# One written order for VectorE and ScalarE over all heads of both halves, with the rotation of q and k in single steps

## The chip, the cores and the metric

The kernel runs on one core of one Trainium2 chip. The metric is the device time of one execution in microseconds. The time before is the median of 3 runs, 2492.38 us (2491.7 to 2492.94).

## What is computed

One decoder layer, batch 1, 1024 tokens, width 2048, all in float32. The reference, cut to what matters:

```python
hn = rmsnorm(h, norm_mix_g[i])
proj = hn @ w_in[i]                       # 2048 -> 8 x 1024 columns
sb_q, sb_k, sb_v, sb_g, df_q, df_k, df_v, df_g = jnp.split(proj, split_at, axis=-1)
# 8 stick-breaking heads: w = sigmoid(z) * prod over later keys of (1 - sigmoid(z)), out = w @ v
# 8 differential heads: rotary on a quarter of each q/k half, (softmax1 - lam * softmax2) @ v, rmsnorm
mixed = jnp.concatenate([sb_out * silu(sb_g), df_out * silu(df_g)], axis=-1)
h = h + mixed @ w_out[i]
gate = sigmoid(rmsnorm(h, norm_ple_g[i]) @ w_ple_gate[i])
h = h + gate * (p[i] @ w_ple_proj[i])
return rmsnorm(h, norm_final_g)
```

## The kernel before

**Products.** Every large product keeps float32 accuracy with two float32r parts of each operand, a high one (a copy) and a low one (the float32 value less the copy). Each product is three matmuls into one accumulator: high by high (L226), high by low (L227), low by high (L228). So each piece of weights costs ScalarE a copy (`whi`, L148), VectorE a subtraction (`wlo`, L149), and each block of the input the same (`xh` L1058, `xl` L1059).

**Stages.** The tokens are cut in two halves of 512 (half 1 holds the tokens that see half the keys). First the v and gate columns of the stick-breaking heads are made by a seven-product scheme (`Seven`, to about 340 us of the span). Then comes the head loop (L1048 to L1186, to about 1711 us): half 1, then half 0, each over heads 8 to 15 (differential) and then 0 to 7 (stick-breaking). Then follow the output projection, again by seven products, and the gated embedding.

**The head loop.** A `unit` (L212) is 4 pieces of weights by 2 column blocks by 4 input blocks: 32 ticks of three matmuls, into the accumulators `acc0` (done at tick 28) and `acc1` (done at tick 32). A differential head has two units (q and k, then v and gate), a stick-breaking head one (q and k; v and gate are loaded). The attention of a head runs beside the units of the next head. The class `Side` holds a list of steps with due ticks; `side.tick()` after each tick emits those that are due, in the order of their due times. `attention` returns such steps: `weights` (scores z by TensorE, mask L312, then for a stick head two sigmoids L328 and L329, a running product L335 and a product L340; for a differential head max L350, exponent L353, scaling L361, difference L366), `turn` (transposes, L398), `parts` (high copies L416 and L417, low subtractions `lead` L421 and `awl` L422), `mix` (the products with v, L440 to L445), `norm` (L485 to L497).

**Who sets the order.** TensorE's order is written by hand throughout. VectorE's and ScalarE's order is written by hand in the seven-product stage (`man2`) and in the stick-breaking heads of half 0 (`man3`, L1081). There `side.written` is true, and `side.later(dt, fn)` makes a step of its own of what else would be emitted at once. In all other heads (half 1, and the differential heads of half 0) the two engines are ordered by the compiler's scheduler from its own estimates. Each engine takes its instructions in order: one that waits holds all behind it.

**Names that the prediction uses.** `taken(c)` evicts accumulator c of q and k (`qk<-acc`, L1092 in stick heads, L1121 and L1123 in differential ones). In the written stick heads `taken(0)` is due at 28 and `taken(1)` at 31.5. The rotation of a differential head is L1125 to L1128 (shuffle, two products, sum) and then 6 or 8 copies and subtractions (L1132 to L1140), all emitted in one go. `tight` is head 15, the last differential head, whose steps are packed closer so that they end before the stick heads begin. At the change of halves the 16 blocks of the new half's input are loaded and split in one loop (L1054 to L1060) ahead of half 0's first head.

Of the kernel before, what the change touches and what calls it, by code (L numbers as in the profile page):

```python
# [13 lines left out]
F32 = mybir.dt.float32  # L14
# [6 lines left out]
P = 128  # L21
# [16 lines left out]
NORM_LAT = 11  # L38
LAM0 = 0.8 - 0.6 * math.exp(0.0)
# [8 lines left out]
def _body(ctx, nc, tc, ap):  # L48
# [226 lines left out]
    def attention(at, pz, half, hd, q, qz, K, KL, VV, sg, vf):  # L275
# [41 lines left out]
        def weights(rb, c):  # L317
# [30 lines left out]
            def one():  # L348
                mx = at.tile([P, 1], F32, name="mx", tag="mx", bufs=8)
                V.reduce_max(mx, z[:, vw], axis=AX.X, negate=True)  # L350
                et = at.tile([P, S], F32, name="et", tag="pt" if c else "bt", bufs=2 if c else 3)
# [75 lines left out]
        def mix(pr, g):  # L427
# [51 lines left out]
            side.later(4, low)  # L479

        def norm(pr):
# [20 lines left out]
            side.later(3, step)  # L502
# [12 lines left out]
        elif tight and half == 0:  # L515
            ss, t0, t1, tv, gap = [[0, 2], [4, 7], [10, 13], [30, 33]], 18, 42, 9, 4
        else:
            s0, s1, s2, t0 = ([0, 1], [3, 5], [7, 9], 16) if tight else ([0, 2], [5, 8], [12, 15], 19)
            gap = 4 if tight else gap
            last = t0 + gap * (n0 - 1)  # L520
            s3 = [last + 1, last + (3 if tight else 5)]
            ss = [s0, s1, s2, s3]
            t1 = s3[-1] + (13 if tight else LATD[half])
            tv = s1[-1] + 2
# [12 lines left out]
    with tc.tile_pool(name="at", bufs=2) as at, tc.tile_pool(name="pz", bufs=2, space=PSUM) as pz:  # L537
# [509 lines left out]
        side.add([(4, norms)])  # L1047
        for half in (1, 0):  # L1048
            tsl = slice(half * HALF, half * HALF + HALF)
            X = {}  # L1050
            if half == 1:
                X = X1
            else:
                for kt in KT:  # L1054
                    hi = xp.tile([P, HALF], F32R, name=f"xh{kt}", tag=f"xh{kt}")
                    lo = xp.tile([P, HALF], F32R, name=f"xl{kt}", tag=f"xl{kt}")
                    nc.sync.dma_start(lo.bitcast(F32), h_d[0, kt])
                    A.activation(hi, lo.bitcast(F32), AF.Copy, scale=gcol(kt))  # L1058
                    V.scalar_tensor_tensor(lo, lo.bitcast(F32), gcol(kt), hi.bitcast(F32), op0=ALU.mult, op1=ALU.subtract)  # L1059
                    X[kt] = hi, lo  # L1060
# [3 lines left out]
            for hd in (ORDER0, ORDER1)[half]:  # L1064
# [5 lines left out]
                if half == 0 and hd == H + 1:  # L1070
                    with tc.issue_after(lastsig[0].ins):
                        A.preload_act_table_set("natural_log_exp_and_others")
# [7 lines left out]
                if half == 0 and hd == 0:  # L1080
                    man3 = tc.manual_schedule(engines={V.engine, A.engine})  # L1081
                    man3.__enter__()
                    side.written = True
                if sb:
                    acc = [pp.tile([P, HALF], F32, name=f"acc{c}", tag="acc", bufs=2) for c in range(2)]
                    qk = [at.tile([P, 2, HALF], F32R, name="q", tag="q"), at.tile([P, 2, HALF + P], F32R, name="k", tag="k")]
                    rstd = rstds[half]

                    def taken(c, acc=acc, qk=qk, rstd=rstd):
                        f = f32t("qk")  # L1090
                        t = qk[c]
                        V.tensor_tensor(f, acc[c], rstd, op=ALU.mult)  # L1092
                        side.later(1, lambda: A.copy(t[:, 0, :HALF], f))
                        side.later(2, lambda: V.tensor_tensor(t[:, 1, :HALF], f, t[:, 0, :HALF].bitcast(F32), op=ALU.subtract))
# [3 lines left out]
                    unit(X, acc=acc, mid={2: load_vg})  # L1098
                    if not side.written:
                        taken(0)  # L1100
                        taken(1)
                    q, k = qk
                else:
                    acc = unit(X)
                rstd = rstds[half]
                if not sb:
                    q = at.tile([P, 2, HALF], F32R, name="q", tag="q")
                    k = at.tile([P, 2, HALF + P], F32R, name="k", tag="k")
                qz = None
                if not sb:  # L1110
                    if nqz[0] % 8 < 2:

                        qzs[nqz[0] % 2] = at.tile([P, 2, HALF], F32R, name="qz", tag="qz")
                        G.memset(qzs[nqz[0] % 2].bitcast(F32), 0.0)
                    qz = qzs[nqz[0] % 2]
                    nqz[0] += 1
                KL = None if sb else at.tile([P, 2, HALF], F32R, name="kl", tag="st")
                for c, t in () if sb else ((0, q), (1, k)):
                    f = f32t("qk")
                    if c == 0:  # L1120
                        V.scalar_tensor_tensor(f, acc[c], DF_SCALE, rstd, op0=ALU.mult, op1=ALU.mult)  # L1121
                    else:
                        V.tensor_tensor(f, acc[c], rstd, op=ALU.mult)  # L1123
                    sw = f32t("sw")
                    V.stream_shuffle(sw, f, SWAP)  # L1125
                    V.tensor_tensor(sw, sw, cs[:, 1, :], op=ALU.mult)
                    V.tensor_tensor(f, f, cs[:, 0, :], op=ALU.mult)
                    V.tensor_tensor(f, f, sw, op=ALU.add)  # L1128
                    for b in range(2):
                        r = slice(64 * b, 64 * b + 64)  # L1130
                        ro = slice(64 - 64 * b, 128 - 64 * b)
                        A.copy(t[r, b, :HALF], f[r])  # L1132
                        if c == 0:
                            A.copy(qz[r, b, :], f[r])
                            V.tensor_tensor(t[ro, b, :], f[r], t[r, b, :].bitcast(F32), op=ALU.subtract)
                        else:
                            A.copy(t[ro, b, :HALF], f[r])
                            V.tensor_tensor(KL[r, 0, :], f[r], t[r, b, :HALF].bitcast(F32), op=ALU.subtract)
                            for rr in (r, ro):
                                V.tensor_tensor(t[rr, b, HALF:], f[r, 3 * P:], t[r, b, 3 * P:HALF].bitcast(F32), op=ALU.subtract)  # L1140

                if sb:
                    vf, gf = vacc = vg
                else:
                    vacc = unit(X)
                    vf, gf = f32t("vf"), f32t("gf")
# [3 lines left out]
                def normed(i, t, vacc=vacc, rstd=rstd):  # L1150
                    V.tensor_tensor(t, vacc[i], rstd, op=ALU.mult)

                def gate(sg=sg, gf=gf, fast=fast):
# [6 lines left out]

                side.later(5, partial(normed, 0, vf))
                side.later(6, partial(normed, 1, gf))
                side.later(7, gate)
                side.later(10, lambda sg=sg, gf=gf: V.tensor_tensor(sg, sg, gf, op=ALU.mult))
                K = [k]
                VV = []
                if half == 1:
                    G.dma_start(k_d[hd].rearrange("p (a b) -> p a b", a=2), k[:, :, 0:HALF])
                    if not sb:
                        G.dma_start(kl_d[hd - H], KL[:, 0, :])  # L1170
                else:
# [17 lines left out]
        man3.__exit__(None, None, None)  # L1189
# [492 lines left out]
```

## Time and profile before

| what | value |
|---|---|
| median of 3 runs | 2492.38 us |
| the profiled execution's own time | 2487.77 us |
| its span, first to last instruction | 2486.0 us |
| mean granted TensorE clock | 0.994 |
| units of half 1, differential heads | about 337 to 734 us |
| units of half 1, stick-breaking heads | about 734 to 960 us |
| units of half 0, differential heads | about 960 to 1420 us |
| units of half 0, stick-breaking heads | about 1420 to 1711 us |

The busy rows of the page count the union of each engine's instructions. TensorE's matmuls overlap: one of 512 columns is shown with 0.39 us, and the next starts 0.227 us after it, so a busy share of 100% says only that no gap was longer than the overlap. A row of the view of waits names the waiting instruction and what released it, the total, the number of waits and the longest. In the timeline a row shows start, duration, engine, line, operation and tiles, and in brackets the idle time before it and what ended that. Back to back, VectorE's next instruction starts about 0.08 us before the end that the row of the one before shows, ScalarE's about 0.10 us, so the step from start to start is the duration less that.

### The profile page before, as it was taken

The page shows a single profiled execution, that of the slowest core. Times are in us where ns is not written, and L with a number is a line of the kernel's source. Part 1 is how long each engine was busy: PE and PEld are TensorE (multiplying, and loading weights), DVE is VectorE, ACT ScalarE, POOL GpSimd, SP SyncE. Part 2 cuts the span into 40 slices and gives each one's busy share as a digit, 9 for nine tenths or more (in the row PEclk, how much of TensorE's full clock was granted, in tenths as well). Part 3 has the DMA queues.
Part 4 walks back from the last instruction along what each step waited for, and adds up shares of the span by engine and source line. Part 5 has one row for each costly group of instructions (what it writes and reads, how often), then busy time and mean ns, then how long its engine had stood idle before and what let it go on. Part 6 is the DMA issues. An engine that isn't in the chain of part 4 may idle for free.

```text
span 2486.0 us, 31946 instructions
## 1 busy us (share of the span) xinstructions
PE 2404.7 (97%) x11434; PEld 1997.5 (80%) x11434; DVE 1794.5 (72%) x3010; ACT 1207.2 (49%) x2064; POOL 279.3 (11%) x361
## 2 busy tenths in 40 slices
PE   7999999999999999999999999998899999999997
PEld 5787878888888887888888878886787887787886
DVE  6888776778777778787878778878678674546555
ACT  5234344555565445555555555445423234546443
POOL 1211110000000001000000001110111113330110
PEclk9999999999999999999999999999999999999999
DMA  8786655444444556344444435556746777343433
GB/s 292 251 269 220 221 180 159 151 146 128 147 136 140 186 161 198 109 123 114 123 115 115 111 102 136 144 135 192 224 167 220 168 188 230 121 131 103 133 109 102
DMA packets 167471, 397.72 MB, mean 160 GB/s; under 512 B 18896, under 2 KB 23248, under 8 KB 167312
## 3 DMA queue, kind: packets, MB, share of 16 engines
q1 hardware_dynamic: 131040, 302.07, 38.3%
q0 software_dynamic: 36272, 93.60, 14.3%
q8 instruction: 90, 1.47, 0.3%
q14 instruction: 69, 0.57, 0.1%
HBM read 297.03 MB, written 106.95 MB: 163 GB/s over the span
## 4 chain that ended last, share of the span: by engine, by line
PE 81%; DVE 8%; DMA 5%; ACT 4%; issue 3%; SPq 0%; DVEq 0%; ACTq 0%
PE acc L226 16%; PE acc L227 16%; PE acc L228 16%; PE pbc L598 4%; PE pbc L596 4%; PE pbc L597 4%; PE tp L398 2%; PE pa L596 1%; PE pa L598 1%; PE pa L597 1%; PE z L305 1%; PE z L304 1%; PE av L445 1%; PE av L444 1%; PE av L443 1%
## 5 line engine op out<-in xcount | busy, mean ns | idle before, releaser
L226 PE MATMUL acc<-xh,whi 128*128 128x512 f32 x1568 | 628.8, 401 | 2.2 <-DVE gt L1295 1.5
L228 PE MATMUL acc<-xh,wlo 128*128 128x512 f32 x1568 | 613.9, 392 | 0.0
L227 PE MATMUL acc<-xl,whi 128*128 128x512 f32 x1568 | 613.5, 391 | 0.0
L149 DVE TENSOR_TENSOR wlo<-wraw,whi 128x1024 fp32r<-128x1024 f32 x252 | 312.6, 1240 | 230.4 <-ACT whi L148 224.8
L148 ACT CAST whi<-wraw 128x1024 fp32r<-128x1024 f32 x252 | 265.0, 1052 | 290.2 <-PE acc L227 255.8
L228 PEld LDWEIGHTS acc<-xh,wlo 128*128 128x128 f32 x1568 | 295.0, 188 | 63.6
L226 PEld LDWEIGHTS acc<-xh,whi 128*128 128x128 f32 x1568 | 296.0, 189 | 57.0 <-issue 2.2
L227 PEld LDWEIGHTS acc<-xl,whi 128*128 128x128 f32 x1568 | 296.2, 189 | 53.5 <-issue 0.2
L686 ACT CAST wpr<-T 128x512 fp32r<-128x512 f32 x128 | 78.1, 621 | 314.4 <-DVE T L644 310.1
L417 ACT CAST awh<-tp 128x256 fp32r<-128x256 f32 (+1 forms) x160 | 81.0, 506 | 108.7 <-PE tp L398 108.6
L353 ACT ACTIVATE et<-z,mx 128x512 f32<-128x512 f32 (+7 forms) x128 | 94.5, 738 | 61.3 <-DVE mx L350 55.3
L110 POOL TENSOR_TENSOR ssq<-ssq,sq 128x512 f32<-128x512 f32 x56 | 83.6, 1493 | 303.6 <-ACT sq L109 253.9
L422 DVE TENSOR_TENSOR awl<-tp,awh 128x256 fp32r<-128x256 f32 (+1 forms) x160 | 92.3, 577 | 31.5 <-ACT awh L417 30.7
L335 DVE TENSOR_TENSOR_SCAN st<-pt 128x511 f32<-128x511 f32 (+3 forms) x64 | 86.7, 1355 | 29.6 <-ACT pt L328 29.1
L350 DVE TENSOR_REDUCE mx<-z 128x1 f32<-128x512 f32 (+7 forms) x128 | 96.4, 753 | 1.4
L700 DVE TENSOR_TENSOR wpr<-T,wpr 128x512 fp32r<-128x512 f32 x128 | 87.7, 685 | 6.3 <-ACT wpr L686 4.5
L596 PE MATMUL pbc<-cS,wpr 128*128 128x512 f32 x224 | 87.5, 390 | 3.2 <-DVE u L1439 1.6
L598 PE MATMUL pbc<-cS,wpr 128*128 128x512 f32 x224 | 87.3, 390 | 0.0
L597 PE MATMUL pbc<-cS,wpr 128*128 128x512 f32 x224 | 87.3, 390 | 0.0
L328 ACT ACTIVATE pt<-z 128x512 f32<-128x512 f32 (+3 forms) x64 | 41.7, 651 | 89.6 <-DVE z L312 81.1
L445 PE MATMUL av<-awl,v 128*128 128x256 f32 x256 | 73.6, 287 | 7.6 <-DVE awl L422 7.6
L226 PE MATMUL acc<-cA11h,whi 128*128 128x512 f32 x192 | 76.2, 397 | 0.6 <-DVE qk L1092 0.6
(402 smaller groups left out, 5335.9 us busy)
## 6 DMA issues: line engine op xcount, KB each, us to landing
wraw<-w_in SPq DMA_DIRECT2D x192, 512.0 KB, 3.6
wraw<-w_gate SPq DMA_DIRECT2D x64, 512.0 KB, 3.6
wraw<-w_out SPq DMA_DIRECT2D x72, 256.0 KB, 3.6
wraw<-w_vg SPq DMA_DIRECT2D x71, 256.0 KB, 4.2
comb_d<-sg POOLq DMA_DIRECT2D x48, 256.0 KB, 7.1
spare<-xT SPq DMA_DIRECT2D x44, 256.0 KB, 3.9
xl<-h_d SPq DMA_DIRECT2D x40, 256.0 KB, 5.1
vghalf_d<-hc POOLq DMA_DIRECT2D x32, 256.0 KB, 4.3
```

The source lines that it names most:

```text
L148: side.later(1, lambda: A.copy(hi[:, o], raw[:, o]))
L149: side.later(4, lambda: V.tensor_tensor(lo[:, o], raw[:, o], hi[:, o].bitcast(F32), op=ALU.subtract))
L226: T.matmul(acc[c], hi[:, k2, kh, c, :], xh, start=first, stop=False)
L227: T.matmul(acc[c], hi[:, k2, kh, c, :], xl, start=False, stop=False)
L228: T.matmul(acc[c], lo[:, k2, kh, c, :], xh, start=False, stop=last)
L350: V.reduce_max(mx, z[:, vw], axis=AX.X, negate=True)
L353: A.activation(et[:, vw], z[:, vw], AF.Exp, bias=mx[:, 0:1], accum_out=l)
L422: V.tensor_tensor(wl[:, o, :], tp[:, o, :], wh[:, o, :].bitcast(F32), op=ALU.subtract)
L445: T.matmul(av, vv[:, 0, blk % 4, :], wl, start=False, stop=last)
L596: T.matmul(o, wh[:, w], xh, start=start and k == 0, stop=False, skip_group_check=True)
L597: T.matmul(o, wh[:, w], xl, start=False, stop=False, skip_group_check=True)
L598: T.matmul(o, wl[:, w], xh, start=False, stop=k == 3, skip_group_check=True)
```

## The change

All head-loop work of VectorE and ScalarE gets the written order: `man2` is no longer closed before the head loop but after it, `man3` goes, and `side.written` is set before the first head. What was emitted at once becomes steps:

- The rotation of a differential head becomes seven steps each for q and k at the due ticks `ROPE`, counted from the eviction; the last of q falls 15.5 ticks and the last of k 23 ticks after it. The two blocks of 64 rows have one step each for their low parts. q and k tiles are allocated at the eviction.
- A differential head's max and exponent are separate steps (`DF`).
- `wlo` is emitted at 3 in place of 4 after the piece's load.
- `taken(1)` is due at 31 in every head (before 31.5 in the written stick heads).
- The split of half 0's 16 input blocks is spread over the last unit of half 1: four times four steps, 4.5 ticks apart.
- Head 15 of half 1 gets the steps `[[0, 2], [4, 7], [10, 13], [22, 25]]` with `gap` 5 in place of `[[0, 1], [3, 5], [7, 9], ...]` with `gap` 4.
- The norm factors of both halves become steps at 1 and 3; `low` and `step` of the sub-norm move from 4 to 5 and from 3 to 4.

No arithmetic is added or left out, and the numbers of matmuls and of VectorE's instructions stay. The core of the diff:

```diff
+XLAT = 6
+DF = 1, 1.5, 4, 5.5
+WLO = 3
+ROPE = (1.5, 5, 7, 8.5, 12, 14, 15.5), (1.5, 13, 14.5, 16, 19.5, 21.5, 23)
...
-            side.later(4, lambda: V.tensor_tensor(lo[:, o], raw[:, o], hi[:, o].bitcast(F32), op=ALU.subtract))
+            side.later(WLO, lambda: V.tensor_tensor(lo[:, o], raw[:, o], hi[:, o].bitcast(F32), op=ALU.subtract))
...
-            def one():
+            def top():
                 mx = at.tile([P, 1], F32, name="mx", tag="mx", bufs=8)
                 V.reduce_max(mx, z[:, vw], axis=AX.X, negate=True)
+                side.later(DF[1], partial(one, mx))
...
-            side.later(1, one)
-            side.later(3, two)
+            side.later(DF[0], top)
+            side.later(DF[2], two)
             if c:
-                side.later(4.5, three)
+                side.later(DF[3], three)
...
         elif tight and half == 0:
             ss, t0, t1, tv, gap = [[0, 2], [4, 7], [10, 13], [30, 33]], 18, 42, 9, 4
+        elif tight:
+            ss, t0, t1, tv, gap = [[0, 2], [4, 7], [10, 13], [22, 25]], 17, 33, 9, 5
...
-        man2.__exit__(None, None, None)
+        side.written = True
...
-                rstd_from(ps, 1.0 / NK, eps6, EPS, ssa[hf], t)
+                side.later(1 if hf else 3, partial(rstd_from, ps, 1.0 / NK, eps6, EPS, ssa[hf], t))
...
+                    def swap(pc):
+                        for i, kt in enumerate((pc * 2, pc * 2 + 8, pc * 2 + 1, pc * 2 + 9)):
+                            side.add([(XLAT + 4.5 * i, load_x0(kt))])
+
+                    side.add([(8 * pc + 7, partial(swap, pc)) for pc in range(4)])
...
-                    if side.written:
-                        side.add([(28, partial(taken, 0)), (31.5, partial(taken, 1))])
+                    side.add([(28, partial(taken, 0)), (31, partial(taken, 1))])
+                    side.add([(36, partial(normed, 0)), (37, partial(normed, 1)), (38, gate), (41, gated)])
...
+                        steps = [lambda: V.stream_shuffle(sw, f, SWAP),
+                                 lambda: V.tensor_tensor(sw, sw, cs[:, 1, :], op=ALU.mult),
+                                 lambda: V.tensor_tensor(f, f, cs[:, 0, :], op=ALU.mult),
+                                 lambda: V.tensor_tensor(f, f, sw, op=ALU.add),
+                                 high, partial(low, 0), partial(low, 1)]
+                        side.add(zip(ROPE[c], steps))
...
         side.written = False
-        man3.__exit__(None, None, None)
+        man2.__exit__(None, None, None)
```

More of the change, by code (lines that the diff above doesn't have):

```diff
@@ L478, in mix @@
             side.later(3, squared)
-            side.later(4, low)
+            side.later(5, low)
         def norm(pr):
@@ L501, in norm @@
             side.later(1, roots)
-            side.later(3, step)
+            side.later(4, step)
         n0 = nb // 2
@@ L1079, in _body @@
                 vg = []
[L1080 to L1094, printed above, removed]
-                    if side.written:
-                        side.add([(28, partial(taken, 0)), (31.5, partial(taken, 1))])
[L1098 to L1146, printed above, removed]
+                rstd = rstds.get(half) if half == 0 or hd != ORDER1[0] else ssa[1]
+                qk = {}
+                if half == 1 and hd == ORDER1[-1]:
+                    def swap(pc):
+                        for i, kt in enumerate((pc * 2, pc * 2 + 8, pc * 2 + 1, pc * 2 + 9)):
+                            side.add([(XLAT + 4.5 * i, load_x0(kt))])
+                    side.add([(8 * pc + 7, partial(swap, pc)) for pc in range(4)])
@@ L1147, in _body, with store_k, two_accs @@
+                def store_k(hd=hd, qk=qk, half=half):
+                    if half == 1:
+                        G.dma_start(k_d[hd].rearrange("p (a b) -> p a b", a=2), qk[1][:, :, 0:HALF])
+                        if hd >= H:
+                            G.dma_start(kl_d[hd - H], qk["kl"][:, 0, :])
+                def two_accs():
+                    return [pp.tile([P, HALF], F32, name=f"acc{c}", tag="acc", bufs=2) for c in range(2)]
                 sg = at.tile([P, HALF], F32, name="sg", tag="sg", bufs=3)
@@ L1159, in gate, with gated, taken, low @@
                         A.activation(sg, sg, AF.Exp, scale=-1.0)
[L1161 to L1164, printed above, removed]
+                def gated(sg=sg, vg=vg):
+                    V.tensor_tensor(sg, sg, vg[1], op=ALU.mult)
+                acc = two_accs()
+                if sb:
+                    def taken(c, acc=acc, qk=qk, rstd=rstd, store_k=store_k):
+                        f = f32t("qk")
+                        if c == 0:
+                            t = at.tile([P, 2, HALF], F32R, name="q", tag="q")
+                        else:
+                            t = at.tile([P, 2, HALF + P], F32R, name="k", tag="k")
+                        qk[c] = t
+                        V.tensor_tensor(f, acc[c], rstd, op=ALU.mult)
+                        def low():
+                            V.tensor_tensor(t[:, 1, :HALF], f, t[:, 0, :HALF].bitcast(F32), op=ALU.subtract)
+                            if c:
+                                store_k()
+                        side.later(1, lambda: A.copy(t[:, 0, :HALF], f))
+                        side.later(2, low)
+                    def normed(i, vg=vg, rstd=rstd):
+                        V.tensor_tensor(vg[i], vg[i], rstd, op=ALU.mult)
+                    side.add([(28, partial(taken, 0)), (31, partial(taken, 1))])
+                    side.add([(36, partial(normed, 0)), (37, partial(normed, 1)), (38, gate), (41, gated)])
+                    unit(X, acc=acc, mid={2: load_vg})
+                    while 1 not in qk:
+                        side.tick()
+                    q, k, qz, KL = qk[0], qk[1], None, None
+                else:
+                    def taken(c, acc=acc, qk=qk, rstd=rstd, store_k=store_k):
+                        f, sw = f32t("qk"), f32t("sw")
+                        if c == 0:
+                            t = at.tile([P, 2, HALF], F32R, name="q", tag="q")
+                            if nqz[0] % 8 < 2:
+                                qzs[nqz[0] % 2] = at.tile([P, 2, HALF], F32R, name="qz", tag="qz")
+                                G.memset(qzs[nqz[0] % 2].bitcast(F32), 0.0)
+                            other = qk["qz"] = qzs[nqz[0] % 2]
+                            nqz[0] += 1
+                            V.scalar_tensor_tensor(f, acc[c], DF_SCALE, rstd, op0=ALU.mult, op1=ALU.mult)
+                        else:
+                            t = at.tile([P, 2, HALF + P], F32R, name="k", tag="k")
+                            other = qk["kl"] = at.tile([P, 2, HALF], F32R, name="kl", tag="st")
+                            V.tensor_tensor(f, acc[c], rstd, op=ALU.mult)
+                        qk[c] = t
+                        rows = [(slice(64 * b, 64 * b + 64), slice(64 - 64 * b, 128 - 64 * b)) for b in range(2)]
+                        def high():
+                            for b, (r, ro) in enumerate(rows):
+                                A.copy(t[r, b, :HALF], f[r])
+                                if c == 0:
+                                    A.copy(other[r, b, :], f[r])
+                                else:
+                                    A.copy(t[ro, b, :HALF], f[r])
+                        def low(b):
+                            r, ro = rows[b]
+                            if c == 0:
+                                V.tensor_tensor(t[ro, b, :], f[r], t[r, b, :].bitcast(F32), op=ALU.subtract)
+                                return
+                            V.tensor_tensor(other[r, 0, :], f[r], t[r, b, :HALF].bitcast(F32), op=ALU.subtract)
+                            for rr in (r, ro):
+                                V.tensor_tensor(t[rr, b, HALF:], f[r, 3 * P:], t[r, b, 3 * P:HALF].bitcast(F32), op=ALU.subtract)
+                            if b:
+                                store_k()
+                        steps = [lambda: V.stream_shuffle(sw, f, SWAP),
[4 more added lines that the diff above has]
+                        side.add(zip(ROPE[c], steps))
+                    side.add([(28, partial(taken, 0)), (31, partial(taken, 1))])
+                    unit(X, acc=acc)
+                    vacc = two_accs()
+                    def normed(i, vacc=vacc, vg=vg, rstd=rstd):
+                        vg.append(f32t(("vf", "gf")[i]))
+                        V.tensor_tensor(vg[i], vacc[i], rstd, op=ALU.mult)
+                    side.add([(28, partial(normed, 0)), (31, partial(normed, 1)), (33, gate), (37, gated)])
+                    unit(X, acc=vacc)
+                    q, k, qz, KL = qk[0], qk[1], qk["qz"], qk["kl"]
```

45 lines of the change are left out of this document (20 added, 25 removed).

## The prediction

> **What bounds the kernel now.** I read the page's busy rows first: TensorE covers 97% of the span, VectorE 72%.
>
> ```profile
> span 2486.0 us, 31946 instructions
> ...
> PE 2404.7 (97%) x11434; PEld 1997.5 (80%) x11434; DVE 1794.5 (72%) x3010; ACT 1207.2 (49%) x2064; POOL 279.3 (11%) x361
> ```
>
> The change leaves TensorE's instructions as they are, and their order too except in head 15 of half 1. So it can only remove TensorE's waits or add some. Where they are shows in the busy time by stretch (length, then busy time of TensorE, weight loads, VectorE, ScalarE, GpSimd; granted clock, DMA share, GB/s).
>
> ```profile
> 511.00:561.00 50.00, 50.00 (x241) 41.88 (x240) 38.09 (x85) 28.13 (x57) 1.76 (x3) 1.00 0.45 143
> 1447.80:1451.20 3.40, 3.40 (x12) 2.82 (x11) 1.99 (x4) 1.63 (x2) 2.27 (x3) 0.50 0.85 231
> 1547.00:1582.40 35.40, 34.89 (x190) 29.78 (x190) 28.39 (x39) 16.71 (x27) 3.75 (x5) 1.00 0.51 134
> ```
>
> In half 1's differential heads (first row) TensorE has no gap, and the view of waits lists none from 360 to 730 us or from 1000 to 1440. That is where the rotation stands: **its spreading has no wait to remove**. The third row is one stick head of half 0 with a gap of 0.5 us, the second a stretch at half clock after a long wait. The view of waits from 1440 to 1480 us (waiter, releaser, us in total, times, longest), then that from 1500 to 1700:
>
> ```profile
> PE av L440 <- DVE awl L422: 3.6, 1, 3.6
> PE av L440 <- DVE lead L421: 2.0, 1, 2.0
> ```
> ```profile
> PE av L440 <- DVE lead L421: 5.5, 5, 3.5
> ```
>
> The other waits in reach: 1.2 us at 738 (z L304 on the exponent L353, head 15 of half 1), 0.6 and 1.2 at 789 and 795, 4.0 in six waits at 951 to 996 (the change of halves), 1.0 at 340. From 340 to 1480 they sum to 1.0 + 1.2 + 1.8 + 4.0 + 5.9 = 13.9 us: the most that the change can win by waits, 0.6% of the time.
>
> **Stick heads of half 0: the reordered eviction.** These were already in written order, and the two programs' orders differ here in one point that matters: the eviction of acc1, due at 31 in place of 31.5. VectorE's rows before, in the head from 1534 us:
>
> ```profile
> 1532.10 0.69 DVE L1094 TENSOR_TENSOR q<-qk,q 128x512 fp32r<-128x512 f32 x1 [0.69 <-ACT q L1093]
> 1532.95 0.69 DVE L422 TENSOR_TENSOR awl<-tp,awh 128x512 fp32r<-128x512 f32 x1 [0.16 <-ACT awh L417]
> 1533.92 0.29 DVE L310 TENSOR_TENSOR zm<-z,masks 128x128 f32<-128x128 f32 x1 [0.28 <-PE z L302]
> 1534.24 0.30 DVE L312 TENSOR_TENSOR z<-z,zm 128x128 f32<-128x128 f32 x1
> 1534.60 0.69 DVE L1092 TENSOR_TENSOR qk<-acc,ssa 128x512 f32<-128x512 f32 x1
> 1535.37 1.49 DVE L335 TENSOR_TENSOR_SCAN st<-pt 128x639 f32<-128x639 f32 x1
> ...
> 1538.56 0.68 DVE L422 TENSOR_TENSOR awl<-tp,awh 128x512 fp32r<-128x512 f32 x1
> ...
> 1546.56 0.26 DVE L421 TENSOR_TENSOR lead<-tp,lead 128x128 fp32r<-128x128 f32 x1
> ```
>
> And TensorE's rows for the last matmul into acc1 and the two that wait further down:
>
> ```profile
> 1534.17 0.39 PE L228 MATMUL acc<-xh,wlo 128*128 128x512 f32 x1
> ...
> 1539.90 0.28 PE L445 MATMUL av<-awl,v 128*128 128x256 f32 x1
> ...
> 1546.88 0.39 PE L440 MATMUL av<-lead,v 128*128 128x256 f32 x1 [0.50 <-DVE lead L421]
> ```
>
> In the new order qk of acc1 stands right behind `q`, ahead of `awl`, `zm` and `z`. acc1 ends at 1534.17 + 0.39 = 1534.56, so VectorE, free at 1532.8, stands until 1534.6. Then qk takes a step of 0.60 (0.69 less 0.08), `awl` 0.61, so `zm` starts at 1535.8, `z` at 1536.1, done at 1536.4 in place of 1534.5: **1.9 us late**. Behind that mask wait ScalarE's sigmoid (before at 1534.64) and VectorE's scan, `k`, `wlo` and the second `awl`, back to back. That `awl` would end at 1539.24 + 1.9 = 1541.1, and TensorE wants it at 1539.90: it was 0.66 early and is 1.2 late. From there to `lead` VectorE has two idle gaps (0.85 and 0.51), but each waits for a ScalarE instruction whose own input moves too, so I let them take up nothing. `lead` is then 1.9 late where TensorE already waited; TensorE itself comes 1.2 later, so 0.7 comes on top. Sum 1.2 + 0.7 = **1.9 us a head**. With heads 2 to 5 alike that is 7.6. The first (`lead` at 1512, before just in time by 0.2) gives 1.7. In the last one both waits meet the 3.5 us wait at 1688: its `awl` at 1682 was just in time and is 1.7 late, its `lead` some 0.9: 2.6. Sum 1.7 + 7.6 + 2.6 = +11.9; bounds 0 (delay all absorbed) and 13.3 (seven heads by 1.9).
>
> **Hand-over to the stick heads (1459 to 1476).** Same eviction: before, qk of acc1 (1459.04) stood behind `zm` 1457.20, the mask and a max; now they stand behind it, so the exponent of 1458.78 comes some 2.4 later. `sql`, at whose row TensorE waited 0.3, ends 1.2 to 1.7 later, and the `lead` at 1475 some 0.7. Together +2.2; bounds 0 and 3.5.
>
> **Head 15.** In half 1 the steps are 2 to 3 ticks apart in place of 1 to 2: z is free in time, and the waits from 738 to 746 (1.2 gap, with its short successors 1.8) go: -1.8; bounds 0 and -2. In half 0 `lead` was late by 3.6 because `sql` (1435.74, after 1.33 idle), `wlo` (1.22) and `v` (0.69) stood ahead of the last keys' mask and max; in the new order mask and max stand ahead of `sql`, and the exponent starts about 1.33 + 1.2 = 2.5 earlier, the rest by the later difference L366 behind `wlo`: -3.2; bounds 0 and -3.6. With that wait goes the half-clock stretch behind it: 3.4 us at 0.50 is -1.7. The late sum is -4.9.
>
> **Start and change of halves.** At 337 the copy of the first piece's `whi` now stands behind four copies `xh` (0.72 each), and the second piece's `wlo` behind all six products of both norm factors (0.67 each) in place of three: TensorE would wait some 0.5, 0.8 and 1.7, and loses its 1.0 wait for the squares: +2.0; bounds -1 and +4. At the change of halves the splits (ScalarE 0.72, VectorE 0.74, sixteen each) no longer come in a lump but reach into the first head of half 0, where they stand among the last stick head's sigmoids and `lead`: the old 4 us of gaps (5.1 over the issue step) mostly go, and waits for z, two late blocks, one `wlo` and `lead` of some 7.5 come. +2.4; bounds -5.1 and +5, because it hangs on when loads land (median 5.1 us for this load). The heads of 789 and 795: +0.3; bounds ±1. Entry of the output projection, whose queue is some 0.5 longer: +0.5.
>
> **Steps at no cost.** `wlo` at 3 in place of 4 keeps its place behind `lead` in the stick heads; `low` and `step`, one tick later, feed the sub-norm of differential heads, where TensorE waits for nothing: 0, bound +0.5 each at head 15. SP's order changes by a dozen loads that move a few places, GpSimd's by one; k's stores are issued earlier. SP's longest wait is for `wlo` (901 us in 172 waits), so weights are loaded a piece ahead and a few places hide: 0, except at the change of halves, where it is in the bounds above.
>
> **Differential heads.** Nothing hides a gain here. As to loss: VectorE has 38.1 of 50 us, and the spread steps leave a `wlo` 1.0 us ahead of its use at the least: 0; bound +1 a head.
>
> **Sum** on the profiled execution: 11.9 + 2.2 - 1.8 - 4.9 + 2.0 + 2.4 + 0.3 + 0.5 = +12.6, taken as +13. That execution took 2487.77 us (span 2486.0 and 1.8 around it), 4.6 below the median of 2492.38; the median after is then **2505 us**.
>
> **A rule on the clock.** In this trace the granted clock is 0.50 for 3.4 us after the wait of 3.6 at 1443 and after that of 2.0 at 1473, and stays at 1.00 after 3.5 at 1688 and after 1.4 at 951. [...]
>
> **Rivals.**
> (1) *Faster: standing at the head of the queue reaches nobody.* Place: everything behind the acc1 eviction, the late `whi` and the spread splits. It decides by the slack ahead of TensorE's use: 0.66 us at `awl` (1539.90), nothing at `lead`. If VectorE and ScalarE made up all delays, only the removals stay: -1.8 - 4.9 - 5.1 = -11.8, 2481 us. Against it: the rows are back to back from 1534 to 1541. 8%.
> (2) *The delay runs out in the two gaps* of 0.85 and 0.51 us: six heads by 1.36 less, 2505 - 8 = 2497, on the border of what counts. For it: the gaps are there; against it: both end on ScalarE rows that move. 10%.
> (3) *The differential heads get waits,* one us in each of fifteen: 2520. For it: VectorE at 76% and in fixed order; against: 1 us of room. 7%.
> (4) *Half clock after the new waits:* eight waits of about 2 us, 1.7 each: 2519. For: the stretch after 2.0 us; against: none after 1.4 and 3.5. [...] 7%.
> The forecast keeps 68%.
>
> **Range and chances.** 2496 to 2516 reaches down to (2) and, upward, to the high bounds of hand-over and change of halves (+1.3 and +2.6) with the rule's 1.7 and some of the differential heads' loss; it leaves out (1), half of (3) and (4), and some edge. A measurement can tell about 0.2% (5 us). Faster 8% from (1); within 5 us 6%, half of (2) and 1% of the forecast; slower 86%.
>
> **What would show it.** Right: `av L440 <- DVE lead` in 1500 to 1700 grows from 5.5 to about 11 us, a new `av L445 <- DVE awl` appears there with some six waits of 1 to 2, the 3.6 us at 1443 is gone, and stretches of the differential heads stay at 50.00 of 50. Wrong: `awl` and `lead` waits unchanged in the stick heads, or gaps among the differential heads.

## The result, and the profile after

The changed kernel takes **2506.17 us** (median of 4 runs, 2502.95 to 2508.74), the kernel before on the same chip 2492.66 (4 runs): ratio 1.0052, 95% interval 1.0035 to 1.0069, so 13.5 us or 0.5% slower. The forecast was 2505. The profiled execution took 2504.36 us. Its busy rows, from the page of the changed kernel:

```profile
span 2502.6 us, 31959 instructions
...
PE 2411.7 (96%) x11434; PEld 1998.8 (80%) x11434; DVE 1810.6 (72%) x3010; ACT 1200.0 (48%) x2063; POOL 279.8 (11%) x361
```

The same numbers of matmuls and of VectorE instructions, 16.6 us more span: what was added is waiting, and some half clock. VectorE's 16 us more are no added work: the durations of its instructions sum to 1942.2 us before and 1941.5 after, but they overlap the end of the one before by 130.9 us in all, where it was 147.6. The busy time by stretch of the changed kernel (length, TensorE, weight loads, VectorE, ScalarE, GpSimd; granted clock, DMA share, GB/s) shows where:

```profile
511.00:561.00 50.00, 50.00 (x241) 41.87 (x240) 39.24 (x86) 27.67 (x56) 1.76 (x3) 1.00 0.45 143
...
1538.70:1576.00 37.30, 35.43 (x190) 29.81 (x190) 28.22 (x39) 16.72 (x27) 3.75 (x5) 1.00 0.48 127
1700.40:1707.20 6.80, 5.51 (x18) 4.74 (x19) 4.52 (x6) 0.99 (x2) 0.00 (x0) 0.50 0.37 101
```

The differential heads (first row) still have no gap. One stick head of half 0 (second row) now needs 37.3 us for the same 190 matmuls, of which TensorE is shown busy for 35.4; before it was 35.4 with 34.9. The third row is a stretch at half clock that the kernel before did not have there. The view of waits of the changed kernel from 1440 to 1480 us, then from 1500 to 1720:

```profile
PE av L447 <- DVE awl L429: 4.1, 2, 2.8
PE msq L492 <- ACT sqh L476: 1.3, 1, 1.3
```
```profile
PE av L447 <- DVE lead L428: 11.6, 6, 5.4
PE av L452 <- DVE awl L429: 5.3, 6, 1.4
```

The wait of 3.6 at 1443 is gone (now 1.25); in the stick heads `lead` has grown from 5.5 to 11.6, and there are six new waits for `awl`: the two rows that the forecast asked for. VectorE's timeline of the changed kernel in the head from 1533 us shows the mechanism, and TensorE's rows the two waits:

```profile
1533.28 0.69 DVE L1134 TENSOR_TENSOR qk<-acc,ssa 128x512 f32<-128x512 f32 x1 [1.80 <-PE acc L232]
1533.89 0.68 DVE L429 TENSOR_TENSOR awl<-tp,awh 128x512 fp32r<-128x512 f32 x1
1534.48 0.28 DVE L314 TENSOR_TENSOR zm<-z,masks 128x128 f32<-128x128 f32 x1
...
1539.13 0.68 DVE L429 TENSOR_TENSOR awl<-tp,awh 128x512 fp32r<-128x512 f32 x1
...
1547.12 0.26 DVE L428 TENSOR_TENSOR lead<-tp,lead 128x128 fp32r<-128x128 f32 x1
```
```profile
1539.87 0.39 PE L452 MATMUL av<-awl,v 128*128 128x256 f32 x1 [0.87 <-DVE awl L429]
...
1547.44 0.50 PE L447 MATMUL av<-lead,v 128*128 128x256 f32 x2 [1.00 <-DVE lead L428]
```

VectorE stands 1.80 us with the eviction at the head of its queue, until acc1 ends; `awl`, `zm` and all that follows come behind it, and TensorE waits 0.87 for the second `awl` and 1.00 for `lead`, where before it waited 0.50 in all.

**Where the time went.** TensorE's order is the same in both programs but for some matmuls of head 15, so the start of the same matmul can be compared. Chosen ones (us in the trace before, after, and the difference):

| matmul at | before | after | difference |
|---|---|---|---|
| end of the first seven products | 336.9 | 338.1 | +1.2 |
| first differential head | 361.7 | 363.8 | +2.1 |
| end of the differential heads of half 1 | 734.9 | 737.0 | +2.1 |
| first stick head of half 1 | 753.3 | 753.6 | +0.3 |
| second | 797.3 | 796.2 | -1.1 |
| first differential heads of half 0 | 1022.6 | 1022.2 | -0.4 |
| behind head 15's last `lead` | 1452.8 | 1448.4 | -4.3 |
| end of the hand-over | 1497.1 | 1493.1 | -4.0 |
| behind the first stick head | 1534.4 | 1533.1 | -1.3 |
| behind four more | 1676.2 | 1682.4 | +6.2 |
| in the last one | 1695.7 | 1708.2 | +12.5 |
| in the output projection | 1792.8 | 1809.2 | +16.4 |

The first +1.2 was there before the head loop, in a stage whose order the change leaves alone: 0.6 of it by 43 us, behind a stretch at half clock at 24 us that lasted 6.8 us in place of 3.4, the rest from 173 to 178 us.

### The profile page after: what moved, and what is told of

Its sections match the earlier page's. It is cut to its first block, busy times and chain, and to the rows that moved or that the text cites. A ratio compares the mean times of both kernels' runs of the same rounds, so it can differ in the third digit from the quotient of the medians.

```text
span 2502.6 us, 31959 instructions
## 1 busy us (share of the span) xinstructions
PE 2411.7 (96%) x11434; PEld 1998.8 (80%) x11434; DVE 1810.6 (72%) x3010; ACT 1200.0 (48%) x2063; POOL 279.8 (11%) x361
## 3 DMA queue, kind: packets, MB, share of 16 engines
q0 software_dynamic: 36272, 93.60, 14.2%
## 4 chain that ended last, share of the span: by engine, by line
PE 79%; DVE 10%; DMA 4%; ACT 4%; issue 3%; SPq 0%; DVEq 0%; ACTq 0%
PE acc L230 16%; PE acc L232 16%; PE acc L231 16%; PE pbc L606 4%; PE pbc L604 4%; PE pbc L605 4%; PE tp L405 2%; PE pa L606 1%; PE pa L604 1%; PE pa L605 1%; PE z L309 1%; PE z L308 1%; PE av L452 1%; PE av L451 1%; PE av L450 1%
```

## The experiments

**1. The eviction alone, from both sides.** First the changed kernel with the one number put back (in both halves' stick heads), then the kernel before with the one number changed:

```diff
-                    side.add([(28, partial(taken, 0)), (31, partial(taken, 1))])
+                    side.add([(28, partial(taken, 0)), (31.5, partial(taken, 1))])
```

> The changed kernel with one number put back: the stick heads' eviction of acc1 due at 31.5 in place of 31 (both halves). Theory: that eviction, at the head of VectorE's queue before acc1 is done, is what costs the stick heads of half 0 (+7.6 in four heads, +6.3 in the last, of +16.6 in all). Then `awl` and `lead` waits from 1500 to 1720 us fall from 5.3 and 11.6 us to about 0 and 5, and the time falls by 8 to 13 us, to 2493 to 2498. Rival: the stick heads lose to the whole of the new order around them (loads, weights' low parts a tick earlier, gate's product as steps of their own), of which the eviction is only one: then the waits stay above 12 us together and the time above 2503.

> The kernel before with that one number changed: 31 in place of 31.5 in the written stick heads of half 0, nothing else. Theory: the whole cost of the stick heads comes with it, so the time rises by 8 to 14 us, to 2500 to 2507, with an `awl` wait of some 0.9 and a `lead` wait of some 1.0 in each of the four middle heads. Rival: alone it costs nothing, because the order around it is the old one: 2492 to 2494 and `lead` still 5.5 us in 5 waits.

Measured: 2495.41 us, ratio to the kernel before 1.0006 (0.9995 to 1.0017); and 2506.99, 1.0059 (1.0046 to 1.0071). The waits from 1500 to 1720 us of the changed kernel with 31.5, then of the kernel before with 31:

```profile
PE av L447 <- DVE lead L428: 7.9, 6, 3.7
...
PE av L452 <- DVE awl L429: 0.7, 2, 0.4
```
```profile
PE av L440 <- DVE lead L421: 10.0, 5, 6.0
PE av L445 <- DVE awl L422: 5.7, 6, 1.4
```

The `awl` waits come and go with that number. By the same matmuls, each of the four middle heads becomes 1.87 us shorter in the one and 1.9 us longer in the other. Half 1's stick heads do not move by 0.1 us. The theory holds: without this number the whole rest of the change, in sum, costs nothing and wins nothing. One thing did not go as expected: `lead` fell to 7.9 and not to 5, and the hand-over's waits (4.1 and 1.3 at 1440 to 1480) stayed.

**2. The rotation in one go.**

```diff
-ROPE = (1.5, 5, 7, 8.5, 12, 14, 15.5), (1.5, 13, 14.5, 16, 19.5, 21.5, 23)
+ROPE = (1, 1, 1, 1, 1, 2, 2), (1, 1, 1, 1, 1, 2, 2)
```

> The changed kernel with q's and k's rotation not spread: the seven steps of each due within two ticks of the eviction, in place of 15.5 and 23. Theory: spreading removes no wait of the kernel before, which had none there, but it is what lets a fixed order have none. Emitted in a lump of some 17 VectorE instructions in a queue of fixed order, the lump stands ahead of the next `wlo` parts and of the mask; then new waits of TensorE for `wlo` come in every differential head, of 2 to 6 us, in all 30 to 65 us: 2535 to 2570. Rival: VectorE, busy 76%, makes it up before TensorE comes: 2504 to 2509, no waits from 360 to 730 us.

Measured: 2607.85 us, 1.0467 (1.0448 to 1.0485): 102 us more than the changed kernel, well above the expected range. Its waits from 360 to 730 us, and two stretches of one of its heads:

```profile
PE acc L232 <- DVE wlo L153: 39.3, 7, 5.8
```
```profile
425.00:430.30 5.30, 0.53 (x3) 0.11 (x1) 5.07 (x13) 3.28 (x7) 0.57 (x2) 1.00 0.00 0
430.30:437.10 6.80, 5.77 (x15) 4.61 (x16) 3.63 (x7) 2.14 (x4) 1.18 (x3) 0.50 0.92 277
```

In the first stretch TensorE stands, no DMA moves, and VectorE is busy for 5.07 of 5.30 us: it works off the lump, with `wlo` behind it. In the second the clock is 0.50 for 6.8 us. Each of the eight heads of half 1 loses 64.0 / 8 = 8.0 us, 5.7 by the wait and most of the rest by the clock. The clock was left out of the expectation; and the waits came at its upper end in every head of half 1 (in seven heads of half 0 they are 2.8). So the spreading has no wait of the kernel before to remove, but in a fixed order it is what keeps 100 us of waits and half clock away.

**3. The weights' low part at 4.** `WLO = 4` in place of 3 in the changed kernel.

> The changed kernel with the weights' low part due 4 ticks after the load in place of 3, as before. Theory: it costs nothing, as predicted, because a piece has 8 ticks (some 5.5 us) until its low part is used, and behind or ahead of one tick's steps makes no wait: 2502 to 2508. Rival: the earlier `wlo` stands ahead of the critical mask steps at the hand-over and change of halves, so that the later one wins 3 to 6 us: 2500 to 2503; or it comes too late in the differential heads: above 2510 with waits for `wlo` from 360 to 730 us.

Measured: 2501.73 us, 1.0036 (1.0022 to 1.005). The total lies in the rival's range, but not for its reason: at the hand-over the later `wlo` loses. By places it is not nothing: +2.6 at 1443 (the wait is 2.25 in place of 1.25, with half clock behind it), +1.6 at 1475 (half clock), +3.1 at 970 (a wait of 3.6 for `wlo`), which is made up by 985, and -2.27 at 1510 in the first stick head. VectorE's rows there, of the changed kernel and of this one:

```profile
1506.19 2.29 DVE L339 TENSOR_TENSOR_SCAN st<-pt 128x1023 f32<-128x1023 f32 x1 [0.50 <-ACT pt L332]
1508.39 1.20 DVE L153 TENSOR_TENSOR wlo<-wraw,whi 128x1024 fp32r<-128x1024 f32 x1
...
1510.43 0.28 DVE L428 TENSOR_TENSOR lead<-tp,lead 128x128 fp32r<-128x128 f32 x1
```
```profile
1508.49 2.29 DVE L339 TENSOR_TENSOR_SCAN st<-pt 128x1023 f32<-128x1023 f32 x1 [0.50 <-ACT pt L332]
...
1511.61 0.28 DVE L428 TENSOR_TENSOR lead<-tp,lead 128x128 fp32r<-128x128 f32 x1
...
1512.14 1.21 DVE L153 TENSOR_TENSOR wlo<-wraw,whi 128x1024 fp32r<-128x1024 f32 x1
```

At 3, `wlo` stands between the scan and `lead`. This is what made the first stick head's `lead` late, not the eviction. From 1720 to 1755, in the entry of the output projection, -3.8 come: the changed kernel's wait of 2.05 at 1748 and the half clock behind it are missing there. I did not follow why.

**4. The entry of the output projection.** Built on the changed kernel with 31.5: operand blocks and weights are loaded in the last unit and split by steps, and the written order ends only when no step is left.

```diff
-        side.written = False
-        man2.__exit__(None, None, None)
...
+                        side.add([(9 + 4.5 * i, partial(early, "A11", i, 6, 7.5)) for i in range(4)])
+                        side.add([(18 + 1 * i, partial(early, "A12", i, 10 + 1 * i, 11.5 + 1 * i)) for i in range(4)])
...
         while side.q:
             side.tick()
+        side.written = False
+        man2.__exit__(None, None, None)
```

> The changed kernel with the stick heads' eviction at 31.5 and the written order kept up through the entry of the output projection: its first operand blocks (A11, then A12) and its first two pieces of weights are loaded in the last unit, and their high and low parts become steps with due ticks, where before all of them were emitted at once behind the last unit. Theory: what the last stick head and the entry lose (before: waits of 3.5 at 1688 and some 10 us more up to 1760; changed kernel: 5.4 and more, with half clock behind) comes from ScalarE standing for the load of `cA11l` ahead of the last head's sigmoid. Then the `lead` wait of the last head falls to about that of the other heads, 0.5 to 1, and the time falls by 5 to 12 us against the same kernel without this edit, to 2483 to 2490. Rival: the waits there come from the chain of the last head itself (scores, sigmoid, scan), which nothing lies beside any more: less than 2 us, 2493 to 2496.

Measured: 2483.67 us, 0.9961 (0.9948 to 0.9975). ScalarE's rows ahead of the last head's sigmoid, in the kernel before, the changed kernel and this one:

```profile
1687.61 0.62 ACT L584 CAST cA11h<-cA11l 128x512 fp32r<-128x512 f32 x1 [1.48 <-DMA cA11l<-mixed_d]
1688.13 1.02 ACT L328 ACTIVATE pt<-z 128x1024 f32<-128x1024 f32 x1
```
```profile
1692.05 0.62 ACT L592 CAST cA11h<-cA11l 128x512 fp32r<-128x512 f32 x1 [1.76 <-DMA cA11l<-mixed_d]
...
1695.57 0.62 ACT L592 CAST cA11h<-cA11l 128x512 fp32r<-128x512 f32 x1 [2.22 <-DMA cA11l<-mixed_d]
...
1697.49 1.02 ACT L332 ACTIVATE pt<-z 128x1024 f32<-128x1024 f32 x1 [0.27 <-DVE z L316]
```
```profile
1688.54 1.03 ACT L332 ACTIVATE pt<-z 128x1024 f32<-128x1024 f32 x1 [1.29 <-DVE z L316]
```

In both kernels ScalarE stands for a load of the next stage, and the sigmoid of the running head waits behind it. In this one the sigmoid waits for its own mask alone, the last head's `lead` wait is 0.5 in place of 3.7, and from 1682 to 1797 us the same matmuls come 14.2 us closer together than without the edit (3.4 of that are two stretches at half clock, at 1692 and 1760, that no longer come; 1.5 are lost again by 1800, to one at 1788 that does). The theory holds for the running head: by 1696 us its shorter wait and the clock behind it make 4.8 of the 14.2. The rest comes in the entry itself, where the edit also loads the weights earlier; what of that each part brings was not separated.

**5. Head 15, and the ticks of the sub-norm**, each put back in the changed kernel: the old `ss` with `gap` 4 for half 1; `low` at 4 and `step` at 3.

> The changed kernel with head 15 of half 1 on its old, tighter steps (gap 4 in place of 5). Theory: the -1.8 us that the changed kernel gains from 734 to 755 us come from the wider steps alone, so they come back: the wait of z for the exponent near 738, of some 1.2, and +1.5 to +2.5 us in all. Rival: the written order of the exponent alone takes that wait away, and the wider steps do nothing: 0 to +0.5.

> The changed kernel with the two steps of the sub-norm back at 4 and 3 in place of 5 and 4. Theory, as predicted: the gain of 3.9 us in head 15 of half 0 (3.6 us wait at 1443) comes from the written order, with the mask and max ahead of `sql`, and the one tick costs nothing; the wait there stays under 2.5 us and the whole within +2 us. Rival: the tick is what puts `sql` behind the mask, so the wait at 1443 is 3.6 again, +2.4 and half clock behind it, +4 in all; or the earlier steps stand ahead of a `wlo` in the differential heads, with waits of some 0.3 in each.

Measured: 2514.78 us (1.0084, 1.007 to 1.0098) and 2512.66 (1.0076, 1.0063 to 1.0088). The first brings +1.4 from 737 to 753 us, with a wait of 0.8 for the exponent: nearly what was expected. The second changes nothing at 1443 (a wait of 1.26): the gain there is the written order's, the rival falls. But the tick does move `sql`, as VectorE's rows of the changed kernel and of this one show:

```profile
1435.50 0.29 DVE L316 TENSOR_TENSOR z<-z,masks 128x128 f32<-128x128 f32 x1
...
1436.70 0.41 DVE L482 TENSOR_TENSOR sql<-sqv,sqh 128x256 fp32r<-128x256 f32 x1
```
```profile
1439.64 0.42 DVE L482 TENSOR_TENSOR sql<-sqv,sqh 128x256 fp32r<-128x256 f32 x1
...
1440.85 0.29 DVE L316 TENSOR_TENSOR z<-z,masks 128x128 f32<-128x128 f32 x1
```

With the old ticks `sql` stands ahead of the mask again, as in the kernel before, and the wait is as short as with it behind: the place of `sql` is not what took the 3.6 us away. No differential head has a wait in either. But both lose 3 to 5 us where nothing was expected, in the first stick head of half 1. Its waits from 740 to 805 us with the sub-norm's old ticks:

```profile
PE z L300 <- ACT bt L333: 1.0, 1, 1.0
PE acc L232 <- DVE wlo L153: 0.5, 1, 0.5
PE acc L230 <- ACT whi L152: 0.4, 1, 0.4
```

With the changed kernel's own ticks there is none of them; behind them comes half clock at 788. With head 15's old steps the waits that the kernel before had at 789 and 795 are there (1.2 for `qk`, 0.7 for `awl`). So in the written order this place, which I had left at +0.3, is free only with the wider steps and the later tick together. The rest of both totals (1.6 to 1.7 each, at 350, 985 and 1475 us with the old steps, at 350, 1475 and 1515 with the old ticks) is half clock behind waits that the changed kernel has as well, and passed at full clock.

**6. The split block by block.** Both blocks' low parts in one step.

```diff
-ROPE = (1.5, 5, 7, 8.5, 12, 14, 15.5), (1.5, 13, 14.5, 16, 19.5, 21.5, 23)
+ROPE = (1.5, 5, 7, 8.5, 12, 14, 14), (1.5, 13, 14.5, 16, 19.5, 21.5, 21.5)
```

> The changed kernel with the low parts of both 64-row blocks of q (and of k) in one step, at the tick of the first block, in place of one step for each block 1.5 ticks apart. Theory: the block-by-block split costs and wins nothing, since the second block's subtraction (some 0.6 us) only changes places with the mask and max of one block, and the differential heads have about 1 us of room: 2503 to 2509, no waits from 360 to 730 us. Rival: 0.6 us more ahead of the mask, or three more k subtractions ahead of a `wlo`, use up the room: waits of 0.2 to 0.6 in the 15 differential heads, 2509 to 2516.

Measured: 2507.37 us, 1.0059 (1.0045 to 1.0073), no waits from 360 to 730: the theory holds, this part of the change is worth nothing by itself.

**7. What delays the hand-over.** The changed kernel with 31.5, `WLO = 4` and `DF = 1, 0.4, 4, 5.5` (exponent in the tick of its max).

> The changed kernel with the eviction at 31.5, the weights' low part at 4, and the differential heads' exponent in the tick of its max in place of half a tick later. It settles what delays the hand-over to the stick heads, which the eviction put back left as it was. Theory: two small moves: the exponent as a step of its own stands behind the copies of `k` and `whi` (1456.28 in place of some 1453.8 on ScalarE), and `wlo`, a tick earlier, stands ahead of the last mask (1.12 us) and, in the first stick head, twice ahead of `lead`'s chain. Then the wait for the high squares (1.3 at 1463) and the wait of 2.2 for `lead` at 1509 go, and one of 1.0 comes at 1443: about 2.5 us faster than with the eviction alone, 2490 to 2494. Rival: the order at the hand-over is set by the chain of masks alone, and the waits at 1463 and 1509 stay: 2494 to 2497.

Measured: 2498.94 us, 1.003 (1.0018 to 1.0041). At the places named the theory holds: the wait for the high squares falls from 1.3 to 0.2, the first stick head's `lead` wait of 2.2 is gone (-2.27). The wait of 2.8 for `awl` at the end of the hand-over stays, and the next one for `awl` is 1.4 in place of 0.7. The total was missed, because the same two moves make waits elsewhere: 3.6 for a `wlo` at 970 with 6.8 us of half clock, 0.24 (0.46 by the same matmuls) for `awl` in seven heads of half 0, and 3.4 at 1447, almost the old 3.6. With `wlo` alone put back this wait is 2.25 (experiment 3). So it is the exponent's own step, together with the earlier `wlo`, that took the 3.6 us wait of the kernel before away.

**8. All edits that won.** Eviction at 31.5, the entry as in 4, `WLO = 4`, norm factors at 6 and 14, splits 2 ticks apart, and v and gate later:

```diff
-                    side.add([(36, partial(normed, 0)), (37, partial(normed, 1)), (38, gate), (41, gated)])
+                    side.add([(39, partial(normed, 0)), (40, partial(normed, 1)), (42, gate), (46, gated)])
```

> The edits together: eviction of acc1 at 31.5 in the stick heads, weights' low part at 4, the entry of the output projection in written order, the norm factors at 6 and 14 ticks in place of 1 and 3, the splits at the change of halves 2 ticks apart in place of 4.5, and the stick heads' v and gate by the norm factor at 39 and 40, sigmoid at 42, product at 46 in place of 36, 37, 38 and 41, so that these stand behind `lead` and its mask rather than ahead. Theory: each of the terms is a matter of place in a queue, so they add: 11 (eviction) and 5 to 12 (entry) and some 5 for the rest against the changed kernel, 2473 to 2486, faster than the kernel before by 0.3 to 0.8%. Rival: a step that is moved out of one wait makes another, so that not more than the first edit's gain is left: 2490 to 2495.

Measured: **2472.84 us**, ratio 0.9917 (0.9904 to 0.9931): faster than both kernels, 0.2 below the expected range. Its busy row, and its waits from 1500 to 1720 us:

```profile
PE 2407.7 (97%) x11434; PEld 1999.1 (81%) x11434; DVE 1809.2 (73%) x3010; ACT 1199.0 (49%) x2063; POOL 279.3 (11%) x361
```
```profile
PE av L447 <- DVE lead L428: 1.4, 7, 0.2
PE pa L606 <- DVE wfl L1087: 0.5, 1, 0.5
PE pa L604 <- ACT wfh L1087: 0.3, 1, 0.3
```

`lead` is at 1.4 us in seven waits, from 11.6. Against the changed kernel with 31.5 alone the start wins 1.3, the change of halves 5.0 (961 to 985 us) and the rest mostly the entry. It also gives back 2.6 at 1443, where the later `wlo` costs the same as in experiment 3, and 4.0 behind 1797 us, with half clock for 6.8 us. Norm factors, the distance of the splits, and v and gate were not run alone, so their shares are read from places.

## Why the prediction was right, and where it was not

The time, the sign and the main mechanism were right. That the total came within 1.2 us of the forecast was in part luck, as the terms show. By the terms of the sum (predicted, then measured by the start of the same matmuls):

- **Four middle stick heads: +7.6, measured +7.55**, 1.89 a head. Experiment 1 shows from both sides that the eviction is the cause. Rivals (1) and (2) fall: the delay reached `lead` in full, the two idle gaps took up nothing.
- **First `lead`: +1.7, measured +2.65, for another reason.** The step that failed is "`wlo` at 3 in place of 4 keeps its place behind `lead` in the stick heads": in the first one it does not, and there it costs 2.27 (experiment 3). With the eviction put back the wait stays at 2.2.
- **Last stick head: +2.6, measured +6.3.** A mis-sized term: I added up VectorE's delay alone. ScalarE there also stands for the load of `cA11l` (1.76 and 2.22 us of idle ahead of the sigmoid), which comes later in the changed kernel: the waits there cost 3.8. And the clock falls to half for 6.8 us in the 5.4 us wait and behind it, which costs 2.5 more.
- **Entry of the output projection: +0.5, measured +3.9**, mis-sized likewise: waits of 11.4 us between the same matmuls (1708 to 1809), 9.2 before, and 1.7 by the clock at 1748. Experiment 4 shows that splits standing ahead of the running head are one cause.
- **Hand-over: +2.2, measured +0.35.** The waits came (+1.9), but 1.6 of half clock that the kernel before had at 1475 did not. The cause was only half right: in the order of before the eviction alone does cost 2.5 there (experiment 1, the kernel before with 31), but in the changed kernel the waits stay with the eviction put back. That of 1.25 for the high squares stays with `wlo` at 4 alone (experiment 3) and falls to 0.2 with the exponent moved too (experiment 7); that of 2.8 for `awl` outlasts both, and its cause is open.
- **Head 15: -1.8, measured -1.83** in half 1; **-4.9, measured -3.9** in half 0, where a wait of 1.25 was left and not 0.4. Experiment 5 puts the first down to the wider steps. In the second the step that failed is "mask and max stand ahead of `sql`": with `sql` ahead of the mask the wait is 1.26 (experiment 5), with it behind 3.44 (experiment 7). What shortened it is the earlier `wlo`, which then stands ahead of the last difference (1441.49, 1442.64) and not between it and `lead` (1.0 of it), and the exponent's own step (some 1.2); by which path the exponent's step does so was not followed.
- **Start: +2.0, measured +0.95** (the wait for the squares, 1.0, went; one of 1.8 for `wlo` at 351 came). **Change of halves: +2.4, measured +0.7**, in its bounds. Neither was tested by a run of its own. **Heads of 789 and 795: +0.3, measured -1.35**: I did not see that the wider steps and the later sub-norm free these as well.
- **Differential heads: 0, measured 0.0** over fifteen heads; rival (3) falls. Experiment 2 shows what keeps it so.

The errors (+0.95, +3.7, +3.4, +1.0 against -1.85, -1.05, -1.7, -1.65) largely took each other out, which is luck and not accuracy: 2.8 together, with 1.2 from ahead of the head loop the 16.6 of the two traces against 12.6 predicted. The medians differ by 13.5, since the execution profiled before lies 4.9 below its median and that of after 1.8. Rival (4), half clock behind eight new waits, falls: from 330 to 1760 us the changed kernel's clock falls twice, in the wait of 5.4 and behind that of 2.05 at 1748, and the length of a wait alone does not tell whether it falls (last section). No run shows a rule that gives the 1.7 in the range: in and behind the last stick head's wait of 5.4 the clock was 0.50 for 6.8 us, which cost 2.5.

## What to carry to other kernels

In a written order, an instruction that waits for TensorE's last matmul belongs behind everything that is ready in the same tick: half a tick of due time was worth 0.5% here, with no work added. Where a wait sits, read what stands ahead of the late instruction on its own engine, and look for work of the next stage there (a split that waits for a load); that is where most was won. And a move has to be priced at every place where the same step occurs: one tick of `wlo` won 1.0 us at one place and lost 2.3 at another.

## What the runs showed of the hardware

Behind some waits of TensorE the granted clock fell to 0.50, and behind others of like length it stayed at 1.00. All waits of TensorE between 330 and 1760 us in the twelve traces of this case, with those that a stretch at half clock begins in or within 3.5 us behind:

| length of the wait, us | waits | followed by half clock |
|---|---|---|
| 1.0 to 1.7 | 88 | 4 |
| 1.7 to 2.4 | 37 | 17 |
| 2.4 to 3.8 | 26 | 20 |
| 4.7 to 6.3 | 15 | 15, of these 14 for 6.8 us |

A stretch in or behind these waits was 3.4 us long (1.7 lost where TensorE works all through it, as from 1447.8 to 1451.2 us in the kernel before, where it is shown busy for 3.4 of 3.4 us at 0.50) or 6.8. With the rotation in one go, seven heads of half 0 have the same wait of 2.83 to 2.85 us, some 62 us apart: the 1st, 6th and 7th are followed by half clock, the four between not. In the kernel before, the wait of 2.0 us at 1473 was followed by half clock, and that of 3.5 us at 1688 passed at full clock.

So the length alone does not tell which wait is followed by half clock; what does was tested by no run. At 24 us, in a stage whose order the change leaves alone, the clock was 0.50 for 3.4 us in the trace before and for 6.8 in that after, and in experiment 5 half clock of 1.6 to 1.7 us each came behind waits that the changed kernel passed at full clock. A term of this size in one execution's trace says nothing of the change by itself.
